# Low-half rotary scores on 128 rows of TensorE instead of 64

## The chip, the core and the metric

The kernel runs on one core of a Trainium2 chip, in one launch. The metric is the device time of one execution in microseconds (us), the median of several runs. TensorE does the matrix products (PE in the profile, PEld for its weight loads), VectorE (DVE), ScalarE (ACT) and GpSimd (POOL) do the rest, and DMA queues are fed by SyncE (SP), ACT and POOL.

## What is computed

The reference is one layer of a streaming encoder trunk: latent attention, a retention branch, a merge and a convolutional feed-forward, for a prompt of 1024 tokens and for 8 samples of 16 tokens, each with a past of 256. The change is in the attention scores alone, in the part with the rotary key:

```python
def mla_scores(qn, qp, k_nope, k_pe):
    s = jnp.einsum('bqhd,bkhd->bhqk', qn, k_nope) + jnp.einsum('bqhr,bkr->bhqk', qp, k_pe)
    return s.astype(jnp.float32) * MLA_SCALE
```

There are 8 heads. The first product runs over 128 numbers a head, the second, the rotary one, over 64, with one key for all heads. The prompt is masked in chunks of 64 keys; a softmax over the keys and a product with the values follow.

## The kernel before

Every float32 operand is split into a high half, rounded to the format that TensorE takes (fp32r), and a low half, the rest. A product of two such operands is three products: high by high, high by low, low by high. All go through one helper, `mmul` (line 188), so most rows of the profile name that line. They sum up in a bank of PSUM.

The work goes in stages: gates, latent and retention; queries, keys and values; the samples' attention; the prompt's attention; then merge and feed-forward. The two middle ones matter here.

**Rotary operands.** The rotary part has only 64 rows a head, so the query keeps both halves in one block of 128 rows: for an even head the high half lies in rows 0 to 63 and the low half in rows 64 to 127, for an odd head the other way round (`qs`, the third plane of `aq`; `qsp` for the samples). The rotary key lies twice below itself in both of its halves: `ks1` is the key's high half on rows 0 to 63 and again on 64 to 127, `kls` its low half likewise (both planes of `kpe`; `kp[0]` and `kp[1]` for the samples). One product of `qs` and `ks1` over 128 rows therefore gives query high by key high and query low by key high together. The third one, query high by key low, takes from `qs` and `kls` only the 64 rows in which the query's high half lies.

**Prompt's attention** (lines 1043 to 1131). For each head four pairs of 128-query blocks are done in the order 0, 3, 1, 2. For block i the keys are the first 128(i+1). Up to 512 keys they lie in one bank (`sc`), above that in two of half the length each. A block's scores are five products for each bank: three with the non-rotary parts (`ak`, `aq`), then the rotary one on 128 rows and the rotary one on 64 rows, both `sc<-kpe,aq` in the profile. So a head has 12 products on 64 rows: one in each of four blocks, two in a row in each of the other four. After the scores VectorE masks (line 1126), takes the row's maximum (L1058) and later scales by the reciprocal of the sum (L1069), and ScalarE takes the exponential (L1065). The result `ap` is transposed on TensorE (`apt`, L1081), split into halves `apT` (L205 on ACT, L206 on DVE), and multiplied by the values `av` into `apo`. An object `stream` places the steps of a pair behind the scores of later blocks, so that TensorE has scores to do while a softmax runs. The order is fixed when the program is written out, and each engine works through its own list.

**Samples' attention** (lines 894 to 1040). For each of 8 samples the product of the latent past and the key weights is made (`mm<-whi,lT`), and the scores of all heads against 272 keys (`sample`, from line 939): the non-rotary ones into `pn`, the rotary ones into `pp`, again one product on 128 rows and one on 64, `sm<-kp,qsp` in the profile. The next sample's products follow on TensorE.

Of the kernel before, what the change touches and what calls it, by code (L numbers as in the profile page):

```python
# [142 lines left out]


class _Stream:
    """Emits chains of dependent stages between units of matrix products."""

    def __init__(self):
        self.now, self.queue = 0, []
# [23 lines left out]
def _body(tc, d):  # L173
# [13 lines left out]
    def mmul(out, l, r, start, stop):  # L187
        E.matmul(out, l, r, start=start, stop=stop)  # L188
# [5 lines left out]
        mmul(out, ll, rh, False, stop)  # L194

    def behind():
        """What is traced in this block issues behind what ACT and DVE were given before it."""
        block = ExitStack()
        for e in (mybir.EngineType.Activation, mybir.EngineType.DVE):
            block.enter_context(tc.issue_after(next(i for i in reversed(nc.cur_bb.bb.instructions) if i.engine == e)))  # L200
        return block
# [9 lines left out]
    with ExitStack() as top:  # L211
# [105 lines left out]
            E.matmul(pw, ones, ones, start=True, stop=True)  # L317
        warm.close()

# [1 line left out]
        qside = ExitStack()  # L321
        with ExitStack() as ph:
            rows = ph.enter_context(pool("xrows"))
# [21 lines left out]
            def xk(k, t):  # L345
                return tuple(a[:, t * P:(t + 1) * P] for a in xr[k])

            # branch gates
            gside = ExitStack()
            gp = gside.enter_context(pool("gside", side=right))  # L350
            ivb = gp.tile([P, T], F32, name="ivb")
            with ExitStack() as sec:
# [14 lines left out]
                pp = [[mm.tile([P, 512], F32, name="mm") for _ in range(NCH)] for _ in range(2)]  # L367
# [39 lines left out]
                for f in range(2, 13):  # L407
                    gate_out(f, fm_tile(mm, wslot(d["w_gate"][f], D), xr))

            # latent and rope key  # L410
            with ExitStack() as sec:
                wk = sec.enter_context(pool("kvwork", bufs=2))
                mm = sec.enter_context(pool("mm_a", bufs=6, space=PSUM))
# [58 lines left out]
                stream.drain()  # L472
                A.dma_start(s_kpe, kpT.bitcast(F32))

            # retention
            with ExitStack() as sec:
                wk = sec.enter_context(pool("rwork", bufs=2))
                mm = sec.enter_context(pool("mm_b", bufs=4, space=PSUM))
# [109 lines left out]
                stream.drain()  # L588
            gside.close()

            # query latent
            qp = qside.enter_context(pool("qlat", side=right))
            qr = [(qp.tile([P, T], F32R, name=f"qlh{k}"), qp.tile([P, T], F32R, name=f"qll{k}")) for k in range(6)]
            invq = const.tile([P, NT], F32, name="invq")
# [19 lines left out]
                            A.activation(acc[:, cs], ps[c], AF.Square)  # L614
                        split(qr[f][0][:, cs], qr[f][1][:, cs], ps[c], gc(C_QLAT, f))

# [1 line left out]
        with ExitStack() as ph:  # L618
            wx = ph.enter_context(pool("wx2", bufs=2))
            pers = ph.enter_context(pool("pers"))  # L620
# [270 lines left out]

            cside.close()

            # attention of the samples
            with ExitStack() as sec:
                mm = sec.enter_context(pool("mm_s", bufs=4, space=PSUM))
                sm = sec.enter_context(pool("sm_s", bufs=4, space=PSUM))
# [41 lines left out]
                nk = PAST + NS  # L939

                def sample(b, lT, kp, rk):
                    pn = sm.tile([P, 512], F32, name="sm")
                    pp = sm.tile([P, 512], F32, name="sm")
                    for l in range(4):
                        qab = tuple(fl(a[:, l, b]) for a in qa)
                        mm3(pn[:, :nk], qab, tuple(a[:, l] for a in lT), l == 0, l == 3)
                    qb = fl(qsp[:, b])
                    mmul(pp[:, :nk], qb, kp[0], True, False)
                    mmul(pp[:, :nk], qb[0:64], kp[1][0:64], False, True)
                    own = wk.tile([P, P], F32, name="own")  # L950
                    G.memset(own, 0.0)
                    r = raw(d["lat_tm"][b].rearrange("p a c -> p (a c)"), 1024)
                    lt = tuple(wk.tile([P, 2, KVL], F32R, name=f"lt{i}") for i in range(2))
                    split(lt[0].rearrange("p a c -> p (a c)"), lt[1].rearrange("p a c -> p (a c)"), r)
                    yield 2
                    pr = sm.tile([P, 512], F32, name="sm")
                    for t2 in range(2):
                        bcast_cols(rk[:, t2], pr[:, t2 * P:(t2 + 1) * P])
                    rb = wk.tile([P, nk], F32, name="srb", bufs=1)
                    A.copy(rb[:, :PAST], pr[:, :PAST])  # L960
                    G.tensor_copy(rb[:, PAST:], rb8[:, b * NS:(b + 1) * NS])
                    s = wk.tile([P, nk], F32, name="ss_")
                    V.tensor_tensor(out=s, in0=pn[:, :nk], in1=rb, op=ALU.mult)
                    V.tensor_tensor(out=s, in0=pp[:, :nk], in1=s, op=ALU.add)
                    st = wk.tile([P, 4], F32, name="sst")
                    V.tensor_reduce(st[:, 0:1], s, AX.X, ALU.max, negate=True)
                    A.activation(s, s, AF.Exp, bias=st[:, 0:1], accum_out=st[:, 1:2])
                    V.reciprocal(st[:, 2:3], st[:, 1:2])
                    V.tensor_scalar(out=s[:, :PAST], in0=s[:, :PAST], scalar1=st[:, 2:3], scalar2=None, op0=ALU.mult)
                    G.tensor_scalar(out=own[:, b * NS:(b + 1) * NS], in0=s[:, PAST:], scalar1=st[:, 2:3], scalar2=None, op0=ALU.mult)  # L970
                    yield 3
                    pt = sm.tile([P, 512], F32, name="sm")
                    for a in range(3):
                        E.transpose(pt[:, a * P:(a + 1) * P], s[:, a * P:(a + 1) * P] if a < 2 else own, ident)
                    pT = tuple(wk.tile([P, 3, P], F32R, name=f"spT{i}", bufs=1) for i in range(2))
                    done[:] = [split(pT[0], pT[1], pt[:, :CH].rearrange("p (a c) -> p a c", a=3))]
                    yield 1
                    ps = sm.tile([P, 512], F32, name="sm")
                    for a in range(2):
                        mm3(ps, tuple(x[:, a] for x in pT), tuple(x[:, a] for x in lt), a == 0, False)  # L980
                    mm3(ps, tuple(x[:, 2] for x in pT), (ck8h, ck8l), False, True)
                    t1 = wk.tile([P, KVL], F32, name="st1", bufs=1)
                    A.copy(t1, ps)
                    yield 1
                    pt = sm.tile([P, 512], F32, name="sm")
                    for a in range(4):
                        E.transpose(pt[:, a * P:(a + 1) * P], t1[:, a * P:(a + 1) * P], ident)
                    pv = pt.rearrange("p (l h i) -> p l h i", l=4, h=H)
                    own = slice(b * NS, (b + 1) * NS)
                    split(t1T[:, :, :, 0, own], t1T[:, :, :, 1, own], pv)  # L990
# [3 lines left out]
                for b in range(NB):  # L994
# [6 lines left out]
                    kp = tuple(wk.tile([P, nk], F32R, name=f"kp{i}") for i in range(2))  # L1001
# [38 lines left out]
                A.dma_start(s_att[:, :, SEQ:].rearrange("h p c -> p h c"), at8)  # L1040
            pre.close()

# [1 line left out]
        with ExitStack() as ph:  # L1044
            ps_s = ph.enter_context(pool("ps_s", bufs=4, space=PSUM))
            ps_t = ph.enter_context(pool("ps_t", bufs=4, space=PSUM))
# [52 lines left out]
            for h in range(H):  # L1099
                qt = ld.tile([P, 3, SEQ], F32R, name="aq")  # L1100
                kt = ld.tile([P, 2, SEQ], F32R, name="ak")
                vt = ld.tile([P, 2, 8, P], F32R, name="av")
                G.dma_start(qt, s_q[h // 2][:, :, h % 2])
                G.dma_start(kt, s_k[h // 4][:, :, h % 4])
                for i in range(2):
                    G.dma_start(vt[:, i], s_v[h // 4][:, i, :, (h % 4) * P:(h % 4 + 1) * P])
                qh, kh, qs = (qt[:, 0], qt[:, 1]), (kt[:, 0], kt[:, 1]), qt[:, 2]
                vh = (vt[:, 0].rearrange("p a c -> p (a c)"), vt[:, 1].rearrange("p a c -> p (a c)"))
                at = wk.tile([P, SEQ], F32, name="aat")
                order = (0, 3, 1, 2)  # L1110
                for g in order:
                    pm = []
                    for i in (2 * g, 2 * g + 1):
                        nk = (i + 1) * P
                        cs = [(0, nk)] if nk <= 512 else [(0, nk // 2), (nk // 2, nk)]
                        sc = [ps_s.tile([P, 512], F32, name="sc") for _ in cs]
                        qi = slice(i * P, (i + 1) * P)
                        e = slice(64 * (h % 2), 64 * (h % 2) + 64)
                        for n, (l, ks) in enumerate(((qh[0], kh[0]), (qh[0], kh[1]), (qh[1], kh[0]), (qs, ks1), (qs, kls))):
                            for c, (a, b) in enumerate(cs):  # L1120
                                if n < 4:
                                    mmul(sc[c][:, :b - a], l[:, qi], ks[:, a:b], n == 0, False)
                                else:
                                    mmul(sc[c][:, :b - a], l[e, qi], ks[e, a:b], False, True)
                        a, b = cs[-1]
                        V.memset(sc[-1][0:64, b - a - 64:b - a], -1e30)
                        pm.append(soft(i, sc, cs))
                        if i % 2:
                            stream.start(values(h, g, pm, vh, at, g == order[-1]))
                        stream.tick()  # L1130
            stream.drain()

# [1 line left out]
        rp = top.enter_context(pool("rrows", side=right))  # L1134

        def new_rows(mm, w, f0, f1, fill):
# [20 lines left out]
        with ExitStack() as ph:  # L1157
# [37 lines left out]
            layer(mm, "w_oa", 8, lambda k, hi, lo: split(hi, lo, raw(s_att[k], T)), att_out)  # L1195
            layer(mm, "w_out", 8, lambda k, hi, lo: split(hi, lo, xf[k]), res_out)

            # the up projection starts before its norm is known
            hr, (pg, pv) = new_rows(mm, "w_up", 0, NJ, lambda k, hi, lo: split(hi, lo, xf[k], gc(C_FFN, k)))

# [1 line left out]
        with ExitStack() as ph:  # L1202
            wk = ph.enter_context(pool("fwork", bufs=1))
            cn = cst("s_conv", (P, NF, 18), wk)
# [169 lines left out]
```

## Time and profile before

| | |
|---|---|
| median of 3 runs | 2484.79 us (2482.94 to 2485.39) |
| span of the profiled execution, first to last instruction | 2481.9 us |
| products on TensorE (PE), busy | 2453.8 us, 99% |
| VectorE, ScalarE, GpSimd, busy | 53%, 34%, 12% |
| samples' attention, steady part | 1015 to 1130 us |
| prompt's attention | 1149.8 to 1345 us |
| one head of the prompt in the middle of it | 1267.80 to 1292.15 us, 24.35 us |

The profile gives the span of the profiled execution and no other time of it; the median of the runs lies 2.9 us above that span. A busy PE is not a PE at its peak: a product's end in the trace is modelled, and the next one's start may lie before it. What a product costs in a dense stretch is the step from its start to the next one's start. In a row of the time line, "x3" is three instructions of one kind put together, with the start of the first and the time to the end of the last, and "64\*128 64x384" is a product whose weights have 64 rows and 128 columns and which streams 64 rows by 384 columns. In brackets stands the idle time of that engine before the row, and what ended it.

### The profile page before, as it was taken

How to read it: one execution, taken by the hardware profiler on the slowest of the kernel's cores; microseconds unless marked ns; L12 is line 12 of the kernel's file. 1: busy time of each engine (PE TensorE's matmuls, PEld its weight loads, DVE VectorE, ACT ScalarE, POOL GpSimd, SP SyncE). 2: the span in 40 equal slices, each digit the busy share in tenths (PEclk: the TensorE clock that was granted, in tenths of full speed). 3: DMA queues.
4: the chain of work that ended last, by engine and by line, in shares of the span. 5: the costliest groups of instructions: out<-in, count | busy, mean ns of one | idle time of the engine just before them, and what ended most of it. 6: DMA issues, size and time to landing. Idle time of an engine off the chain costs nothing.

```text
span 2481.9 us, 36197 instructions
## 1 busy us (share of the span) xinstructions
PE 2453.8 (99%) x14360; PEld 2327.1 (94%) x14360; DVE 1319.7 (53%) x2779; ACT 836.9 (34%) x2050; POOL 302.0 (12%) x514
## 2 busy tenths in 40 slices
PE   9999999999999999999999999999999999999999
PEld 8999898998999978887888999999999999999999
DVE  5223456446249766445776244346555555555555
ACT  5121332333236545665555122133222122222220
POOL 0001000001013312332110000001110101101010
PEclk9999999999999999999999999999999999999999
DMA  5333220111226676328663342211111111111102
GB/s 199 102 110 111 85 71 20 64 64 37 69 78 181 188 245 207 130 84 234 163 177 105 124 161 91 91 60 43 51 43 43 43 43 35 51 43 43 41 29 84
DMA packets 125273, 238.52 MB, mean 96 GB/s; under 512 B 10000, under 2 KB 73872, under 8 KB 124848
## 3 DMA queue, kind: packets, MB, share of 16 engines
q1 hardware_dynamic: 40320, 125.95, 15.5%
q10 hardware_dynamic: 58256, 62.30, 7.4%
q0 software_dynamic: 26528, 47.95, 7.0%
q8 instruction: 113, 1.85, 0.3%
q14 instruction: 56, 0.46, 0.1%
HBM read 168.76 MB, written 67.42 MB: 95 GB/s over the span
## 4 chain that ended last, share of the span: by engine, by line
PE 95%; DVE 3%; ACT 1%; DMA 1%; issue 1%; POOL 0%; ACTq 0%; SPq 0%; DVEq 0%; POOLq 0%
PE mm L188 81%; PE sm L188 4%; PE sc L188 4%; PE apo L188 2%; PE apt L1081 2%; DVE wlo L206 0%; PE sm L554 0%; PE sm L311 0%; PE sm L691 0%; DVE uqT L697 0%; DMA wraw<-s_att 0%; ACT whi L205 0%; PE sm L859 0%; DMA wraw<-w_gate 0%; DVE uqT L209 0%
## 5 line engine op out<-in xcount | busy, mean ns | idle before, releaser
L205 ACT CAST whi<-wraw 128x1024 fp32r<-128x1024 f32 (+2 forms) x165 | 172.4, 1053 | 725.7 <-PE mm L188 623.9
L188 PE MATMUL mm<-rh,whi 128*128 128x384 f32 x1728 | 393.0, 336 | 1.6 <-ACT rh L205 1.5
L188 PE MATMUL mm<-rh,wlo 128*128 128x384 f32 x1680 | 384.2, 336 | 0.0
L188 PE MATMUL mm<-rl,whi 128*128 128x384 f32 x1632 | 372.7, 336 | 0.1
L188 PEld LDWEIGHTS mm<-rh,whi 128*128 128x128 f32 x1728 | 308.2, 188 | 3.5 <-ACT rh L205 1.7
L188 PEld LDWEIGHTS mm<-rh,wlo 128*128 128x128 f32 x1680 | 300.3, 188 | 0.0
L188 PEld LDWEIGHTS mm<-rl,whi 128*128 128x128 f32 x1632 | 291.1, 188 | 0.4 <-DVE rl L206 0.4
L206 DVE TENSOR_TENSOR wlo<-wraw,whi 128x1024 fp32r<-128x1024 f32 (+2 forms) x165 | 200.1, 1222 | 141.8 <-ACT whi L205 141.8
L188 PE MATMUL mm<-whi,xh 128*128 128x256 f32 (+2 forms) x720 | 228.4, 334 | 0.7 <-DVE gsig L361 0.7
L188 PE MATMUL mm<-whi,xl 128*128 128x256 f32 (+2 forms) x720 | 225.5, 330 | 0.0
L188 PE MATMUL mm<-wlo,xh 128*128 128x256 f32 (+2 forms) x720 | 225.0, 329 | 0.2 <-DVE wlo L206 0.2
L1258 DVE TENSOR_TENSOR xf<-mm,xf 128x384 f32<-128x384 f32 x264 | 131.5, 550 | 86.2 <-PE mm L188 86.2
L1232 DVE TENSOR_TENSOR u<-mm,iv2b 128x384 f32<-128x384 f32 (+1 forms) x126 | 57.1, 507 | 208.9 <-PE mm L188 208.9
L188 PEld LDWEIGHTS mm<-whi,xl 128*128 128x128 f32 x720 | 132.6, 190 | 12.1
L188 PEld LDWEIGHTS mm<-whi,xh 128*128 128x128 f32 x720 | 132.7, 190 | 10.5 <-issue 0.7
L188 PEld LDWEIGHTS mm<-wlo,xh 128*128 128x128 f32 x720 | 132.8, 190 | 9.8 <-DVE wlo L206 0.4
L188 PE MATMUL mm<-xh,whi 128*128 128x384 f32 x528 | 123.6, 340 | 3.8 <-ACT whi L205 3.0
L188 PE MATMUL mm<-xl,whi 128*128 128x384 f32 x528 | 121.9, 336 | 0.0
L188 PE MATMUL mm<-xh,wlo 128*128 128x384 f32 x528 | 121.4, 336 | 0.0
L188 PE MATMUL mm<-ah,whi 128*128 128x384 f32 x480 | 110.5, 336 | 0.0
L188 PE MATMUL mm<-al,whi 128*128 128x384 f32 x480 | 110.4, 336 | 0.0
L188 PE MATMUL mm<-ah,wlo 128*128 128x384 f32 x480 | 109.8, 336 | 0.0
(448 smaller groups left out, 4450.1 us busy)
## 6 DMA issues: line engine op xcount, KB each, us to landing
wraw<-w_up SPq DMA_DIRECT2D x44, 512.0 KB, 3.2
s_q<-uqT ACTq DMA_DIRECT2D x36, 384.0 KB, 3.1
aq<-s_q POOLq DMA_DIRECT2D x8, 1536.0 KB, 9.3
wraw<-w_dn SPq DMA_DIRECT2D x22, 512.0 KB, 3.2
s_gate<-gsig ACTq DMA_DIRECT2D x16, 576.0 KB, 4.9
mg<-s_gate POOLq DMA_DIRECT2D x16, 576.0 KB, 4.6
wraw<-w_rqkv SPq DMA_DIRECT2D x16, 512.0 KB, 3.8
s_v<-kvT ACTq DMA_DIRECT2D x16, 512.0 KB, 4.7
```

What stands on the lines that cost most here:

```text
L188: E.matmul(out, l, r, start=start, stop=stop)
L205: A.copy(hi, src)
L206: return V.tensor_tensor(out=lo, in0=src, in1=hi.bitcast(F32), op=ALU.subtract)
L1081: E.transpose(pt[:, j * 256 + e * P:j * 256 + (e + 1) * P], pm[e][:, jj * P:(jj + 1) * P], ident)
L1232: V.tensor_tensor(out=u[:, 2 + c * CH:2 + c * CH + n], in0=ps[c][:, :n], in1=ivb[:, c * CH:c * CH + n], op=ALU.mult)
L1258: V.tensor_tensor(out=xf[f][:, cs], in0=ps[c], in1=xf[f][:, cs], op=ALU.add)
```

## The change

In both places the last of the five products takes all 128 rows, instead of the 64 on which the query's high half lies. What is added to the scores by it is query low by key low. The number of products is the same, and so are their columns; 104 of them, 96 in the prompt's attention and 8 in the samples', have 128 rows in place of 64. On each engine the instructions stand in the same order in both kernels. Comment lines taken out aside, this is the whole of it:

```diff
@@ sample
                     mmul(pp[:, :nk], qb, kp[0], True, False)
-                    mmul(pp[:, :nk], qb[0:64], kp[1][0:64], False, True)
+                    mmul(pp[:, :nk], qb, kp[1], False, True)
@@ attention of the prompt
                         qi = slice(i * P, (i + 1) * P)
-                        e = slice(64 * (h % 2), 64 * (h % 2) + 64)
                         for n, (l, ks) in enumerate(((qh[0], kh[0]), (qh[0], kh[1]), (qh[1], kh[0]), (qs, ks1), (qs, kls))):
                             for c, (a, b) in enumerate(cs):
-                                if n < 4:
-                                    mmul(sc[c][:, :b - a], l[:, qi], ks[:, a:b], n == 0, False)
-                                else:
-                                    mmul(sc[c][:, :b - a], l[e, qi], ks[e, a:b], False, True)
+                                mmul(sc[c][:, :b - a], l[:, qi], ks[:, a:b], n == 0, n == 4)
```

## Rows read from the trace of the kernel before

**Rows 1.** The profile's page: the busy time of each engine, and the chain of work that ended last, by engine.

```profile
PE 2453.8 (99%) x14360; PEld 2327.1 (94%) x14360; DVE 1319.7 (53%) x2779; ACT 836.9 (34%) x2050; POOL 302.0 (12%) x514
...
PE 95%; DVE 3%; ACT 1%; DMA 1%; issue 1%; POOL 0%; ACTq 0%; SPq 0%; DVEq 0%; POOLq 0%
```

**Rows 2.** Busy time in stretches, in us, with the number of instructions, then the granted clock of TensorE as a share of its full speed, the DMA share and GB/s: the samples' steady part, the prompt's first head, one head in the middle, and the prompt's whole stage.

```profile
1015.00:1130.00 115.00, 115.00 (x565) 94.25 (x563) 45.84 (x111) 72.34 (x294) 39.92 (x74) 1.00 0.25 82
...
1149.80:1174.00 24.20, 24.09 (x149) 19.62 (x148) 18.96 (x63) 12.83 (x41) 2.59 (x4) 1.00 1.29 380
...
1267.80:1292.15 24.35, 24.35 (x158) 20.26 (x158) 18.14 (x59) 14.18 (x43) 3.25 (x4) 1.00 0.64 173
1149.80:1345.00 195.20, 194.75 (x1242) 161.57 (x1242) 145.91 (x466) 112.70 (x336) 20.89 (x26) 1.00 0.63 170
```

**Rows 3.** Groups of weight loads by shape: busy us, mean ns of one, then the idle time of the loading side just before them and what ended it.

```profile
L188 PEld LDWEIGHTS sc<-kpe,aq 128*128 128x128 f32 x96 | 17.7, 188 | 1.3
L188 PEld LDWEIGHTS sc<-kpe,aq 64*128 64x128 f32 x96 | 15.3, 184 | 15.1 <-issue 13.4
```

**Rows 4.** Time line around the block with 384 keys of the head in the middle: first the products from the rotary one on 128 rows on, with the first and the second product of the values behind it (the last row holds the second and the third), then the weight loads of the same stretch.

```profile
1279.82 0.34 PE L188 MATMUL sc<-kpe,aq 128*128 128x384 f32 x1
1280.08 0.44 PE L188 MATMUL sc<-kpe,aq 64*128 64x384 f32 x1
1280.45 0.39 PE L188 MATMUL apo<-apT,av 128*128 128x256 f32 x1
1280.68 0.40 PE L188 MATMUL apo<-apT,av 128*128 128x256 f32 x2
...
1279.64 0.19 PEld L188 LDWEIGHTS sc<-kpe,aq 128*128 128x128 f32 x1
1280.08 0.18 PEld L188 LDWEIGHTS sc<-kpe,aq 64*128 64x128 f32 x1 [0.25 <-issue]
1280.45 0.76 PEld L188 LDWEIGHTS apo<-apT,av 128*128 128x128 f32 x6 [0.19 <-ACT ap L1065]
```

**Rows 5.** Time line of the products around the block with 768 keys of the same head (two banks of 384), from the second rotary product on 128 rows to the first transposes; the last row begins with the second transpose.

```profile
1287.43 0.34 PE L188 MATMUL sc<-kpe,aq 128*128 128x384 f32 x1
1287.69 0.44 PE L188 MATMUL sc<-kpe,aq 64*128 64x384 f32 x1
1287.97 0.34 PE L188 MATMUL sc<-kpe,aq 64*128 64x384 f32 x1
1288.24 0.33 PE L1081 MATMUL apt<-ident,ap 128*128 128x128 f32 x1
1288.40 0.38 PE L1081 MATMUL apt<-ident,ap 128*128 128x128 f32 x2
```

**Rows 6.** The same for the block with 512 keys in one bank: the last two products on 128 rows and, with the one on 64 and the first transpose left out between them, the row that begins with the second transpose.

```profile
1281.71 0.40 PE L188 MATMUL sc<-ak,aq 128*128 128x512 f32 x1
1281.94 0.40 PE L188 MATMUL sc<-kpe,aq 128*128 128x512 f32 x1
...
1282.87 0.38 PE L1081 MATMUL apt<-ident,ap 128*128 128x128 f32 x2
```

**Rows 7.** The same for one sample: its rotary products and the first two products of the next sample's past.

```profile
1080.39 0.29 PE L188 MATMUL sm<-kp,qsp 128*128 128x272 f32 x1
1080.61 0.39 PE L188 MATMUL sm<-kp,qsp 64*128 64x272 f32 x1
1080.93 0.50 PE L188 MATMUL mm<-whi,lT 128*128 128x512 f32 x1
1081.26 0.40 PE L188 MATMUL mm<-wlo,lT 128*128 128x512 f32 x1
```

**Rows 8.** Time line of dense stretches in which all products have 128 rows: three products of 384 columns and the start of the next three (merge stage), 24 products of the values and the scores behind them, and two products of 128 columns with the start of the next.

```profile
1349.79 0.68 PE L188 MATMUL mm<-rh,wlo 128*128 128x384 f32 x3
1350.31 0.68 PE L188 MATMUL mm<-rl,whi 128*128 128x384 f32 x3
...
1288.98 3.00 PE L188 MATMUL apo<-apT,av 128*128 128x256 f32 x24
1291.82 0.50 PE L188 MATMUL sc<-ak,aq 128*128 128x128 f32 x3
...
1267.60 0.39 PE L188 MATMUL sc<-ak,aq 128*128 128x128 f32 x2
1267.82 0.28 PE L188 MATMUL sc<-kpe,aq 128*128 128x128 f32 x1
```

**Rows 9.** Time line of VectorE in the same head: the mask of the block with 1024 keys, the first step after its scores, and the scaling of that block's softmax, the last step before its transposes.

```profile
1277.45 0.11 DVE L1126 MEMSET sc<- 64x64 f32 x1
...
1281.22 0.80 DVE L1069 TENSOR_SCALAR ap<-ap,ast 128x1024 f32<-128x1024 f32 x1
```

**Rows 10.** Waits of the loading side of TensorE (what it waited for, us in total, times, longest): on VectorE's split of the transposed softmax in the prompt's first head (1149.8 to 1174 us), and the same after the last head's scores (1340 to 1346 us).

```profile
PEld apo L188 <- DVE apT L206: 0.3, 1, 0.3
...
PEld apo L188 <- DVE apT L206: 0.5, 1, 0.5
```

**Rows 11.** Stretches as in Rows 2: before and in a stretch at the lower clock, at the end of the keys' stage, and the samples' last chain.

```profile
985.00:990.40 5.40, 3.42 (x31) 3.22 (x30) 3.24 (x9) 1.78 (x5) 3.32 (x4) 1.00 0.72 243
990.46:1000.70 10.24, 7.66 (x28) 6.57 (x28) 4.81 (x7) 6.13 (x11) 1.81 (x11) 0.50 0.78 244
...
1130.00:1142.50 12.50, 7.63 (x36) 4.88 (x35) 6.66 (x13) 4.19 (x9) 3.88 (x5) 1.00 0.49 164
```

## The prediction

> **What bounds the kernel now.** The page comes first: TensorE is busy for 99% of the span and makes up 95% of the chain that ended last [rows 1]. A busy share says little of an engine whose records overlap, so the second view is the two stages that the change touches, by stretches [rows 2]. In the samples' steady part TensorE is busy for 115.00 of 115 us, in the prompt's stage for 194.75 of 195.20, at the full clock. VectorE comes next: 145.91 of 195.20 us in the prompt's stage, and 18.14 of 24.35 in one head. So time taken off TensorE is taken off the kernel as long as the softmax on VectorE and ScalarE keeps up.
>
> The third view is the weight loads by shape [rows 3]. The 96 loads on 64 rows have 15.1 us of idle time before them, 13.4 of it with nothing that the profile shows to wait for; the 96 on 128 rows, one product earlier, have 1.3. Nothing was late there: TensorE itself stood between two kinds of product.
>
> The fourth view is the time line there [rows 4]. The load for the 128-row product begins at 1279.64, and the product at 1279.82. The 64-row load comes only at 1280.08, 0.25 us after the last load ended, and its product begins in the same moment. The next load, on 128 rows again, waits another 0.19 us, and its product, too, begins with it at 1280.45. The profile puts this second wait down to ScalarE's `ap`, which fits nothing that the values need; the same wait stands before the transposes [rows 5] with no releaser. Both ways across the border, from 128 rows to 64 and back, a load does not start beneath the product before it.
>
> **The change, part by part.** It removes no product and no column. It takes away 72 visits to the other shape: 64 in the prompt (8 heads by 8 blocks; two products on 64 rows in a row are one visit) and 8 in the samples.
>
> *What one visit costs.* I take the time from the start of the last 128-row product to the start of the second product after the visit, less what the same products take where all have 128 rows. The prices for that: 384 columns take (1350.31 - 1349.79) / 3 = 0.173 us, 256 columns (1291.82 - 1288.98) / 24 = 0.118, 128 columns (1267.82 - 1267.60) / 2 = 0.11 [rows 8], and 512 columns 1281.94 - 1281.71 = 0.23 [rows 6].
> - One bank of 384, values behind it [rows 4]: 1280.68 - 1279.82 = 0.86; two products of 384 and one of 256 are 2 x 0.173 + 0.118 = 0.46; the visit costs 0.40.
> - Two banks of 384, transposes behind them [rows 5]: 1288.40 - 1287.43 = 0.97; three of 384 and one of 128 are 0.63; the visit costs 0.34.
> - One bank of 512, transposes behind it [rows 6]: 1282.87 - 1281.94 = 0.93; two of 512 and one of 128 are 0.57; it costs 0.36.
> - A sample [rows 7]: 1081.26 - 1080.39 = 0.87; two of 272 columns, at 0.173 / 384 a column 0.12 each, and one of 512 are 0.48; it costs 0.39.
>
> Half of the prompt's visits have two banks (0.34), half one (0.36 to 0.40, mean 0.38), so I take 0.36: 64 x 0.36 = 23.0 us. The samples give 8 x 0.39 = 3.1. Together 26.1 us on TensorE. The bounds are 72 x 0.34 = 24.5 and 72 x 0.40 = 28.8.
>
> *What the full rows add.* Afterwards the low product has the shape and the weights of the one before it, and that one's step is the price used above, so I add nothing. No row has the new product itself; the bound from above stands with the last rival.
>
> *A rule that speaks against it.* In the rows the load for a 128-row product begins at 1279.64, while the scores before it, on 128 rows as well, still run, and the product follows 0.18 us after the one before, about the bare step for 384 columns [rows 4, 8]. The Trainium skill (TensorE: Matmul & The Clock Gate, Part 3, The mechanism) says instead that a weight load overlaps a running product only where the two use different groups of rows; by it, loads would stay in the open after the change, with the time of the third rival below in place of the forecast. The trace disagrees with it.
>
> *What is not passed on.* The saving counts where TensorE is the one that is waited for. Four places are not so:
> - Each of the seven later heads: the block with 1024 keys is scaled until 1281.22 + 0.80 = 1282.02 [rows 9] and transposed from 1282.87 on [rows 6], a slack of 0.85 us. The chain begins with the mask at 1277.45 [rows 9], and two visits lie between (0.40 and 0.36, [rows 4, 6]), so 0.76 of the 0.85 is eaten. It should just do, but VectorE is the busiest helper there, 18.14 of then some 21.5 us [rows 2]; I take 0.2 a head, 7 x 0.2 = 1.4, between 0 and 7 x 0.76 = 5.3.
> - The first head: VectorE is busier than later, 18.96 of 24.20 us [rows 2], and TensorE already waits for its split, 0.3 us once [rows 10], so part of its 8 x 0.36 = 2.9 goes into that wait; I take 1.0, between 0 and 2.9.
> - The samples' last chain is one of latencies: TensorE is busy for 7.63 of 12.5 us [rows 11]. The eighth visit lies at its start; I take 0.3 of its 0.39 as lost, between 0 and 0.39.
> - Behind the last scores TensorE waits 0.5 us for the split [rows 10]; I take 0.3, between 0 and 0.5.
>
> Together 3.0 us are lost, so 26.1 - 3.0 = 23.1 us are gained: 2481.9 - 23.1 = 2458.8 for the profiled span, and 2484.8 - 23.1 = 2461.7 for the median, which lies 2.9 us above that span. Everything behind the prompt's stage moves up by the same amount: the next rows are split by ScalarE behind its last copy of `apo`, and TensorE waits for them as before.
>
> With the bounds of the visits and of the losses (0 to 9.1), the forecast's own range is 28.8 to 24.5 - 7.0 = 17.5 us of gain, all losses at their worst at once being left out: 2456.0 to 2467.3.
>
> **The rivals.**
> - *The softmax sets the pace.* If VectorE and ScalarE come no faster than now, the block with 1024 keys loses its whole 0.76 in seven heads, and the pair with 640 and 768 keys, which has the next most work on VectorE, as much again: 7 x 1.52 = 10.6 in place of 1.4. Gain 26.1 - 10.6 - 1.6 = 13.9, time 2470.9. For it: VectorE at 75% of the stage, and in order. Against it: it has 6 us of idle time in a head, and its work begins earlier, too. 8%.
> - *The clock falls in the samples' last chain.* The granted clock was 0.50, the lower level of 1.2 GHz, for 10.24 us after a stretch in which TensorE was busy for 3.42 of 5.40 us [rows 11]. The samples' chain, busy for 7.63 of 12.5 us, kept 1.00. It will come 3 us earlier, and its gaps may then fall otherwise. Such a fall would cost at most half of 10.24 us, 5.1: time 2466.8. 6%.
> - *Loads stay in the open.* The load of the low product and the one behind it may go on waiting for the product before them, since they share its rows. Then of each visit two loads of a step of 0.11 remain, 0.36 - 0.22 = 0.14, and 72 x 0.14 = 10.1: time 2474.7. Against it: the 128-row load at 1279.64 [rows 4]. 3%. This is what the Trainium skill's rule, weighed above, would make of it.
> - *The wait doesn't come from the shape* but from the end of a sum in PSUM, which lies at the same product. Then nothing changes: 2484.8. Against it: where the values end and scores begin, both on 128 rows, there is no gap (24 steps of 0.118 reach right to the scores' start, [rows 8]). 3%.
> - *Slower: the wait stays for such a reason, and a product's time goes by its rows.* The 64-row products have 8 x 4608 + 8 x 272 = 39040 columns, at 0.173 / 384 a column 17.6 us; if half the rows had taken half of that, the change adds 8.8 us: 2493.6. It decides wherever a visit gives back less than 8.8 / 72 = 0.12 us. Against it: two 64-row products of 384 columns stand 0.28 us apart [rows 5], not 0.09. 3%.
>
> **How the numbers follow.** The forecast has 77%. Its range to 2467.3 takes in the clock's case as well, 83% together; for the softmax, I stretch it to 2469, short of that rival's full price. A measurement of this kernel can tell 0.2%, 5 us, from no change; all cases but the last two are faster by more: 94% faster, 3% the same, 3% slower.
>
> **What would show it.** In the changed kernel's trace the loads `sc<-kpe,aq` and `sm<-kp,qsp` have one shape each, with 1 to 3 us of idle time before all 192 of the prompt's. The step from the rotary product to the low one is 0.17 to 0.18 us at 384 columns, and one head takes about 24.35 - 2.7 = 21.7 us in place of 24.35. The prompt's stage takes about 195.2 - 20.3 = 175 us, and each sample's period is 0.4 us shorter. The forecast is wrong if waits of TensorE for `ap` or `apT` take over in the middle heads (first rival), if PEclk shows 0.5 near 1130 to 1150 us (second), if the idle time before the low product's load stays (third and fourth), or if its step is longer than that of the product before it (last).

## The result and the profile after

The changed kernel takes 2464.56 us, median of 4 runs (2463.86 to 2468.71), against 2484.02 us for the kernel before, run beside it (2482.94 to 2485.39, 4 runs). The ratio is 0.9925, with a 95% interval from 0.9910 to 0.9939: 19.5 us faster, where 23.1 were forecast. The profiled run took 2464.82 us, its span is 2463.0 us, 18.9 less than before.

The page first: the busy time of each engine, and the chain that ended last. They are the same lines as in [rows 1].

```profile
PE 2435.9 (99%) x14360; PEld 2333.8 (95%) x14360; DVE 1319.5 (54%) x2779; ACT 835.8 (34%) x2050; POOL 302.3 (12%) x514
...
PE 94%; DVE 3%; ACT 1%; DMA 1%; issue 1%; POOL 0%; ACTq 0%; SPq 0%; DVEq 0%; POOLq 0%
```

TensorE is busy for 17.9 us less with the same 14360 products, and the other engines do what they did. The groups of weight loads by shape show where:

```profile
L188 PEld LDWEIGHTS sc<-kpe,aq 128*128 128x128 f32 x192 | 33.5, 188 | 2.6
...
L188 PEld LDWEIGHTS sm<-kp,qsp 128*128 128x128 f32 x16 | 2.5, 188 | 0.0
```

All loads have one shape. In [rows 3] 16.4 us of idle time stood before the prompt's 192; now it is 2.6.

The next rows are the counterpart of [rows 4, 5, 7]: the time line of the block with 384 keys in a head in the middle (products, then loads), of the two banks of 384 in the same head, and of one sample.

```profile
1267.91 0.34 PE L188 MATMUL sc<-kpe,aq 128*128 128x384 f32 x1
...
1268.08 0.35 PE L188 MATMUL sc<-kpe,aq 128*128 128x384 f32 x1
...
1268.38 0.40 PE L188 MATMUL apo<-apT,av 128*128 128x256 f32 x2
...
1267.91 0.19 PEld L188 LDWEIGHTS sc<-kpe,aq 128*128 128x128 f32 x1
...
1268.09 0.19 PEld L188 LDWEIGHTS apo<-apT,av 128*128 128x128 f32 x1
...
1274.49 0.51 PE L188 MATMUL sc<-kpe,aq 128*128 128x384 f32 x2
...
1275.12 0.38 PE L1081 MATMUL apt<-ident,ap 128*128 128x128 f32 x2
...
1046.34 0.29 PE L188 MATMUL sm<-kp,qsp 128*128 128x272 f32 x1
...
1046.83 0.40 PE L188 MATMUL mm<-wlo,lT 128*128 128x512 f32 x1
```

From the rotary product to the low one the step is 0.17 us. From the rotary product to the second product of the values it is 1268.38 - 1267.91 = 0.47 us, where [rows 4] had 0.86 and the forecast's bare steps add up to 0.46. Of the two banks, the row at 1274.49 begins with the second rotary product and the one at 1275.12 with the second transpose: 0.63 us for 0.97 in [rows 5], and again just the bare steps. In the sample it is 0.49 for 0.87 [rows 7]. The loads for the low product and for the values now begin at 1267.91 and 1268.09, each while the product before it runs. A rule that the Trainium skill states (TensorE: Matmul & The Clock Gate, Part 3, The mechanism), that loads overlap running products only where the groups of rows differ, would have them wait; as in the trace of before, these rows say otherwise.

Where the prompt's stage begins and ends, and where two of its heads lie, is read from single products in the time line, in the changed kernel

```profile
1151.36 0.27 PE L188 MATMUL sc<-ak,aq 128*128 128x128 f32 x1
...
1169.54 0.27 PE L188 MATMUL sc<-ak,aq 128*128 128x128 f32 x1
...
1256.81 0.28 PE L188 MATMUL sc<-ak,aq 128*128 128x128 f32 x1
...
1278.53 0.28 PE L188 MATMUL sc<-ak,aq 128*128 128x128 f32 x1
...
1329.16 0.45 PE L188 MATMUL mm<-rh,whi 128*128 128x384 f32 x1 [1.51 <-ACT rh L205]
```

and in the kernel before:

```profile
1149.91 0.27 PE L188 MATMUL sc<-ak,aq 128*128 128x128 f32 x1
...
1169.63 0.28 PE L188 MATMUL sc<-ak,aq 128*128 128x128 f32 x1
...
1347.77 0.44 PE L188 MATMUL mm<-rh,whi 128*128 128x384 f32 x1 [1.51 <-ACT rh L205]
```

The stage, from its first scores to the merge's first product, went from 197.86 us to 177.80, 20.06 less; the forecast had 20.3. The first head takes 18.18 us instead of 19.72, the head in the middle 21.72 instead of 24.35 [rows 2]. Yet the stage **begins later** than before, though the eight samples ahead of it have become shorter. The stretches between them, in the columns of [rows 2], show why: first in the kernel before, from the last sample's first rotary product to the prompt's first scores,

```profile
1129.48:1149.91 20.43, 15.56 (x103) 12.55 (x101) 9.64 (x17) 7.53 (x16) 8.00 (x10) 1.00 0.85 224
```

then in the changed kernel, as a whole and in parts:

```profile
1126.22:1151.36 25.14, 20.11 (x102) 16.49 (x101) 9.79 (x17) 7.54 (x16) 8.01 (x10) 0.73 0.87 232
...
1126.50:1130.00 3.50, 1.90 (x11) 1.34 (x10) 1.80 (x6) 0.91 (x3) 1.01 (x1) 1.00 0.00 0
1130.07:1140.31 10.24, 8.23 (x22) 5.44 (x20) 4.25 (x7) 2.85 (x6) 1.99 (x3) 0.50 0.64 204
1140.31:1143.72 3.41, 1.99 (x15) 1.76 (x16) 0.69 (x1) 0.59 (x1) 2.21 (x3) 1.00 0.98 334
1143.72:1147.13 3.41, 3.41 (x18) 3.41 (x17) 0.42 (x1) 0.37 (x1) 2.80 (x4) 0.50 1.47 310
```

The samples' last chain arrives 3.26 us earlier (2.7 from seven shorter periods; the other 0.5 lie ahead of the samples, where the program is the same) and then takes 4.71 us longer. The granted clock, 1.00 throughout this chain in the kernel before, is 0.50 in 13.65 of these us, the lower level of 1.2 GHz. It fell twice, each time behind a stretch in which TensorE was busy for little more than half (1.90 of 3.50 us, 1.99 of 3.41). The products show the price one by one:

```profile
1130.85 0.63 PE L188 MATMUL sm<-ck8h,spT 128*128 128x512 f32 x1
1131.28 0.63 PE L188 MATMUL sm<-ck8l,spT 128*128 128x512 f32 x1
1131.70 0.63 PE L188 MATMUL sm<-ck8h,spT 128*128 128x512 f32 x1
```

512 columns take 0.43 us from start to start here, and took 0.23 in [rows 6].

So the profile adds up to - 3.26 + 4.71 - 20.06 = - 18.6 us, and 0.3 us more were saved behind the prompt.

### The profile page after: what moved, and what is told of

Its sections match the earlier page's. It is cut to its first block, busy times and chain, and to the rows that moved or that the text cites. A ratio compares the mean times of both kernels' runs of the same rounds, so it can differ in the third digit from the quotient of the medians.

```text
span 2463.0 us, 36197 instructions
## 1 busy us (share of the span) xinstructions
PE 2435.9 (99%) x14360; PEld 2333.8 (95%) x14360; DVE 1319.5 (54%) x2779; ACT 835.8 (34%) x2050; POOL 302.3 (12%) x514
## 4 chain that ended last, share of the span: by engine, by line
PE 94%; DVE 3%; ACT 1%; DMA 1%; issue 1%; POOL 0%; ACTq 0%; SPq 0%; DVEq 0%; POOLq 0%
PE mm L188 81%; PE sm L188 4%; PE sc L188 3%; PE apo L188 2%; PE apt L1081 1%; DVE wlo L206 0%; DMA s<-s_ret 0%; PE sm L554 0%; DVE uqT L697 0%; DMA wraw<-w_gate 0%; PE sm L311 0%; PE sm L691 0%; PE sm L859 0%; DVE uqT L209 0%; PE sm L987 0%
```

## The experiments

The ratio is to the kernel before, run beside each (median 2484.56 us for e1 to e4, 2484.41 for full_again, e5, e8 and e9, 2485.02 for e10), with a 95% interval. "Chain" is the time from the last sample's first rotary product to the prompt's first scores, "stage" from there to the merge's first product, both in the profiled run.

| | median us | runs | ratio | chain | stage |
|---|---|---|---|---|---|
| before (first profile) | | | | 20.43 | 197.86 |
| after (first profile) | 2464.56 | 4 | 0.9925 (0.9910 to 0.9939) | 25.14 | 177.80 |
| full_again: the changed kernel | 2464.39 | 4 | 0.9922 (0.9909 to 0.9935) | 24.86 | 177.80 |
| e1_prompt_only | 2464.33 | 5 | 0.9920 (0.9908 to 0.9933) | 22.02 | 177.81 |
| e2_samples_only | 2486.84 | 11 | 1.0009 (1.0000 to 1.0018) | 26.01 | 197.96 |
| e4_two_visits | 2495.82 | 5 | 1.0045 (1.0031 to 1.0059) | 21.98 | 210.2 |
| e5_second_place | 2487.41 | 11 | 1.0014 (1.0005 to 1.0022) | 20.39 | 200.9 |
| e3_fill | 2462.46 | 4 | 0.9913 (0.9899 to 0.9926) | 22.45 | 178.7 |
| e8_fill_four | 2461.38 | 4 | 0.9910 (0.9897 to 0.9923) | 21.93 | 177.6 |
| e10_fill_three | 2459.79 | 4 | 0.9897 (0.9880 to 0.9913) | 20.12 | 177.78 |
| e9_before_fill | 2484.03 | 12 | 0.9999 (0.9990 to 1.0007) | 20.85 | 197.9 |

### The two parts apart

The prompt's part alone is the changed kernel with the samples' line as before:

```diff
-                    mmul(pp[:, :nk], qb, kp[1], False, True)
+                    mmul(pp[:, :nk], qb[0:64], kp[1][0:64], False, True)
```

> The prompt's low rotary product runs on 128 rows, the samples' one stays on 64. Theory (a visit to the 64-row shape costs TensorE 0.36 us, and the changed kernel lost 4.7 us again because its samples' last chain came 3 us earlier and met the lower clock): the prompt's stage gives its 20 us, the samples' periods stay as in the kernel before, and the last chain of the samples keeps the granted clock of 1.00, so 2484 - 20 = 2464 us, as fast as the full change although only 64 of 72 visits are gone. Rival 1 (the clock falls there whatever the samples do, since the prompt's part or the run decides it): 2468 to 2469 us, with 0.50 near 1130 to 1150 us. Rival 2 (the prompt's saving depends on the samples' stage): another step than 20 us from the prompt's first scores to its last.

The samples' part alone is the kernel before with the opposite edit.

> The samples' low rotary product runs on 128 rows, the prompt's one stays on 64. Theory: each sample's period is 0.39 us shorter, the last chain comes 3 us earlier, the clock falls to 0.50 in it, and 4.7 us are given back: 2484 - 3 + 4.7 = 2485.5 us, no faster or slower than before by 1 to 2 us. Rival (the fall has nothing to do with the samples' shift): clock 1.00 in the chain and 2481 us.

The changed kernel ran once more:

> The changed kernel once more, on the chip of the next two, as their yardstick. Theory: 2464.5 us, with the clock at 0.50 in the samples' last chain in most executions. Rival (that fall was of the one profiled execution): 2460 us and 1.00.

The prompt's part alone gives the whole gain: 2484.56 - 2464.33 = 20.2 us, with a stage as short as in the changed kernel. The samples' part alone gives none: by the medians it is 2.3 us slower (the interval begins at no change), although it makes the seven periods before the chain 2.7 us shorter in all. Its 11 runs lie between 2481.01 and 2490.49 us. The stretches of its profile, from the fall of the clock to the prompt's first scores:

```profile
1129.55:1146.62 17.07, 13.64 (x47) 10.41 (x46) 5.21 (x9) 3.81 (x8) 6.99 (x9) 0.50 0.91 256
1146.62:1151.60 4.98, 4.98 (x45) 4.98 (x45) 2.59 (x4) 2.54 (x4) 0.00 (x0) 1.00 1.63 374
```

Here two thirds of the chain ran at the lower clock, and it took 26.01 us. In the second profile of the changed kernel the clock fell three times, for 3.4 us each:

```profile
1124.81:1128.00 3.19, 1.59 (x11) 1.12 (x10) 1.29 (x4) 1.18 (x4) 1.01 (x1) 1.00 0.00 0
1128.00:1131.42 3.42, 3.42 (x9) 2.19 (x7) 1.41 (x5) 0.61 (x2) 1.25 (x2) 0.50 0.00 0
1131.42:1134.83 3.41, 1.94 (x11) 1.21 (x11) 1.38 (x3) 1.55 (x3) 0.00 (x0) 1.00 0.85 263
1134.83:1138.24 3.41, 3.06 (x7) 1.86 (x7) 2.05 (x2) 0.26 (x1) 0.74 (x1) 0.50 0.92 291
```

(and again from 1141.66 to 1145.07). The chain's 24.86 us are close to the 25.14 of the first profile, with another pattern. In the profile of the prompt's part alone it fell once, behind a longer stretch at the full clock in which TensorE was busy for two thirds:

```profile
1128.52:1142.90 14.38, 9.50 (x49) 6.47 (x48) 6.82 (x13) 4.52 (x11) 5.22 (x7) 1.00 0.52 170
1142.91:1146.33 3.42, 3.42 (x18) 3.42 (x17) 0.42 (x1) 0.37 (x1) 2.77 (x4) 0.50 1.11 374
```

In this kernel nothing ahead of that chain is changed, and its chain takes 1.6 us longer than in the profile of before. So the clock is not wholly a matter of the program. But in the three profiles with the samples' part the chain takes 4.4 to 5.6 us more than the 20.43 of before; in the three more without it (e1, e4, e5), between nothing and 1.6.

These are single executions. The mean granted clock of a whole run is on record for nearly all runs, and though it takes in falls elsewhere, too, it says the same: 0.990 to 0.994 (median 0.992) in the 8 runs of the changed kernel and 0.991 to 0.995 (0.992) in the 11 of the samples' part, but 0.993 to 0.995 (0.995) in the 5 of the prompt's part and 0.993 to 0.997 (0.994) in 45 of the kernel before. The fastest run of the samples' part, 2481.01 us, had 0.995: it is the time that the rival had forecast for a chain at the full clock.

### Is it the number of visits?

Here the kernel before is changed so that the rotary part goes bank by bank, and blocks with two banks have two visits to the 64-row shape instead of one. The products are the same:

```diff
-                        for n, (l, ks) in enumerate(((qh[0], kh[0]), (qh[0], kh[1]), (qh[1], kh[0]), (qs, ks1), (qs, kls))):
+                        for n, (l, ks) in enumerate(((qh[0], kh[0]), (qh[0], kh[1]), (qh[1], kh[0]))):
                             for c, (a, b) in enumerate(cs):
-                                if n < 4:
-                                    mmul(sc[c][:, :b - a], l[:, qi], ks[:, a:b], n == 0, False)
-                                else:
-                                    mmul(sc[c][:, :b - a], l[e, qi], ks[e, a:b], False, True)
+                                mmul(sc[c][:, :b - a], l[:, qi], ks[:, a:b], n == 0, False)
+                        for c, (a, b) in enumerate(cs):
+                            mmul(sc[c][:, :b - a], qs[:, qi], ks1[:, a:b], False, False)
+                            mmul(sc[c][:, :b - a], qs[e, qi], kls[e, a:b], False, True)
```

> The kernel before, with the two banks of a long block done one after the other in the rotary part, so that the two 64-row products of a block are no longer next to each other: 104 visits in place of 72, the same 104 products. Theory (each visit costs 0.34 to 0.40 us): 32 x 0.36 = 11.5 us more, 2495.5 us. Rival (each 64-row product costs, whatever stands beside it, as 26 / 104 = 0.25 us): no change, 2484 us. Second rival (the wait belongs to the end of a sum in a bank): no change either, since each bank's sum ends once in both.

The median rose by 2495.82 - 2484.56 = 11.3 us for 32 more visits, 0.35 us each; the stage of the profile, by 12.3 us, gives 0.38. The groups of loads by shape:

```profile
L188 PEld LDWEIGHTS sc<-kpe,aq 128*128 128x128 f32 x96 | 18.0, 188 | 7.2 <-issue 6.4
...
L188 PEld LDWEIGHTS sc<-kpe,aq 64*128 64x128 f32 x96 | 17.5, 183 | 21.8 <-issue 20.1
```

Before both, the idle time is longer than in [rows 3], and before the 128-row loads it is new: those of the second banks now follow a 64-row product. With the same products and columns as before, the cost goes by the crossings.

### Is it the end of a sum?

Here the 64-row product of the kernel before becomes the second of the five instead of the last:

```diff
-                        for n, (l, ks) in enumerate(((qh[0], kh[0]), (qh[0], kh[1]), (qh[1], kh[0]), (qs, ks1), (qs, kls))):
+                        for n, (l, ks) in enumerate(((qh[0], kh[0]), (qs, kls), (qh[0], kh[1]), (qh[1], kh[0]), (qs, ks1))):
                             for c, (a, b) in enumerate(cs):
-                                if n < 4:
-                                    mmul(sc[c][:, :b - a], l[:, qi], ks[:, a:b], n == 0, False)
+                                if n != 1:
+                                    mmul(sc[c][:, :b - a], l[:, qi], ks[:, a:b], n == 0, n == 4)
                                 else:
-                                    mmul(sc[c][:, :b - a], l[e, qi], ks[e, a:b], False, True)
+                                    mmul(sc[c][:, :b - a], l[e, qi], ks[e, a:b], False, False)
```

> The kernel before, with the prompt's low rotary product still on 64 rows, but as the second of the five products of a block instead of the last, so that the sum in a bank ends with a product on 128 rows. Theory (the wait belongs to the change of shape): still one visit a block, each with products on 128 rows on both sides, 64 x 0.38 in place of 64 x 0.36: 2484.5 + 1 = 2485.5 us, no faster than before. Rival (the wait belongs to the end of a sum in PSUM): the 64-row product no longer lies there, the wait goes with its place and the price of the shape vanishes: up to 20 us less, 2464 us.

It took 2487.41 us, 3.0 more than before. The idle time before the 64-row loads moved with them into the middle of the sum:

```profile
L188 PEld LDWEIGHTS sc<-kpe,aq 128*128 128x128 f32 x96 | 17.7, 188 | 1.3
...
L188 PEld LDWEIGHTS sc<-kpe,aq 64*128 64x128 f32 x96 | 15.4, 184 | 14.2 <-issue 12.7
```

A sum now ends with a product on 128 rows, and nothing was saved. So the end of a sum is not the cause. The 3.0 us appear in the stage as well (200.9 for 197.86), and spread over the 64 visits they are 0.05 us each. In the block with two banks of 384, from the second product on 128 rows to the second one behind the visit:

```profile
1290.00 0.34 PE L188 MATMUL sc<-ak,aq 128*128 128x384 f32 x1
...
1291.09 0.33 PE L188 MATMUL sc<-ak,aq 128*128 128x384 f32 x1
```

These four steps of 384 columns take 1.09 us, 0.40 more than the bare 0.69, where the visit with transposes behind it cost 0.34 in the kernel before. What makes a visit dearer with scores behind it is not shown.

### Giving the clock back

If the samples' last chain lost its time to the clock, and the clock falls behind TensorE's gaps, filling these gaps with products should return it. In what is left of the last two samples' chains, 20 products of 512 columns on operands that lie in SBUF anyway go to spare banks of PSUM; nobody reads their result, and the outputs are the same. The three versions differ in the number of spare tiles N alone:

```diff
                     for t2 in range(2):
                         bcast_cols(rk[:, t2], pr[:, t2 * P:(t2 + 1) * P])
+                        fill(b, 3 - t2)
...
                         E.transpose(pt[:, a * P:(a + 1) * P], s[:, a * P:(a + 1) * P] if a < 2 else own, ident)
+                    fill(b, 3 if b == NB - 1 else 0)
...
                     mm3(ps, tuple(x[:, 2] for x in pT), (ck8h, ck8l), False, True)
+                    fill(b, 3)
...
                         E.transpose(pt[:, a * P:(a + 1) * P], t1[:, a * P:(a + 1) * P], ident)
+                    fill(b, 6 if b == NB - 1 else 0)
...
+                def fill(b, n):
+                    if b >= NB - 2 and spare:
+                        for i in range(n):
+                            mmul(spare[i % N], c8h[:, 0], ck8h, True, True)
...
                     stream.start(sample(b, lT, kp, rk))
+                    if b == NB - 1:
+                        spare.extend(mm.tile([P, 512], F32, name="mm") for _ in range(N))
```

First with one tile:

> The full change, with 20 products of 512 columns whose result nobody reads, put on TensorE in the waits of the samples' last chain. Theory (the gaps of TensorE in that chain bring the clock down): with the gaps filled the granted clock stays at 1.00 from 1126 to 1150 us, and 4 to 4.7 us come back: 2460 us, 4 us faster than the full change. Rival 1 (the fall does not follow TensorE's gaps): 0.50 again, 2465 us. Rival 2 (the filling products, 0.22 us each, delay the chain more than the clock gives back): clock 1.00, but the chain longer by up to 20 x 0.22 = 4.4 us: 2464 us.

It took 2462.46 us. The clock stayed at 1.00 while the chain ran, and fell only behind it:

```profile
1126.00:1129.50 3.50, 3.12 (x17) 2.31 (x15) 1.89 (x6) 0.85 (x2) 1.01 (x1) 1.00 0.00 0
...
1149.64:1153.05 3.41, 3.41 (x11) 3.04 (x10) 1.78 (x7) 0.75 (x4) 0.00 (x0) 0.50 1.08 406
```

The spare tile had also changed which bank of PSUM the prompt's first scores take. TensorE now waited 2.04 us for VectorE's copy (line 1051) of the last of the four sums ahead of them, which stands behind the split of a weight: that sum's bank was the one they took. So the same fills went over four tiles:

> The full change with the same 20 filling products, spread over four tiles in place of one. In the first filled kernel the one tile shifted the order of the PSUM banks behind it, so that the prompt's first scores waited 2.04 us for a bank that VectorE still read, and the clock fell for 3.4 us right there. Theory: with four tiles the banks come in the old order, this wait and this fall go, the chain keeps 1.00, and the whole 4.7 us come back: 2459.5 to 2460.5 us. Rival (the wait is for the first head's key load, which lands no earlier): no gain on the first filled kernel, 2462.5 us.

2461.38 us, with the clock at 1.00 to the end of the chain; the changed kernel beside it took 2464.39. The expectation that the banks would come in the old order did not hold: the wait remained, now on the third of the four sums.

```profile
1126.75:1148.68 21.93, 18.86 (x122) 16.04 (x120) 10.49 (x19) 7.78 (x17) 9.11 (x12) 1.00 0.92 230
...
1148.68 0.33 PE L188 MATMUL sc<-ak,aq 128*128 128x128 f32 x1 [1.53 <-DVE wraw L1051]
```

With three tiles it should be the second sum's bank:

> The changed kernel with the same 20 filling products in the samples' last chain as in the run with four spare tiles, now over three. Nothing else differs; the results of the filling products go nowhere. What moves is the bank in which the prompt's first scores land: with four spare tiles it was the bank of the third sum behind the attention's output weights, whose copy on VectorE stands behind the split of a weight that landed late, and TensorE waited 1.7 us there; with three it is the bank of the second sum, copied some 4 us earlier. Theory: that wait goes and the first scores come right behind the last sums, at the full clock: the time falls from 2461.4 by 1.0 to 1.7 us, to 2459.7 to 2460.4, about what the prediction's terms give without any fall of the clock (2459.9). Rival 1: the second block's scores, which need the bank of the third sum, take the wait over: no change, 2461.0 to 2461.8. Rival 2: the clock falls once behind the chain as in the run with one spare tile: 2462 to 2463, with 0.50 for 3.4 us between 1145 and 1155.

2459.79 us, as the theory had it. The wait is gone; the first row below is the chain's stretch, the others its first product, the first scores and the stage's end:

```profile
1126.35:1146.47 20.12, 18.57 (x123) 15.93 (x121) 9.73 (x17) 7.44 (x16) 8.01 (x10) 1.00 0.85 224
...
1126.35 0.29 PE L188 MATMUL sm<-kp,qsp 128*128 128x272 f32 x1
...
1146.47 0.28 PE L188 MATMUL sc<-ak,aq 128*128 128x128 f32 x1
...
1324.25 0.45 PE L188 MATMUL mm<-rh,whi 128*128 128x384 f32 x1 [1.51 <-ACT rh L205]
```

The chain takes 20.12 us, 5.0 less than in the changed kernel's first profile, at the full clock. This version is faster than both kernels: by 25.2 us than the one before (ratio 0.9897), and by some 4.7 us than the changed one, whose 8 runs lie between 2463.30 and 2468.71 us; the 4 here lie between 2458.14 and 2460.40, though the two did not run side by side.

The control is the kernel before with the fills of e8_fill_four:

> The kernel before with the same 20 filling products on four tiles. Theory (they do nothing but hold the clock, and it was held there already): 2484.5 us, within 1.5 us of before. Rival (the filling itself makes the stage faster or slower, so that the filled kernels say nothing of the clock): off by 3 to 5 us.

2484.03 us, ratio 0.9999: no change, and the chain 20.85 us for 20.43. The 0.4 us more are about the wait for a bank that four tiles bring, 0.46 us here.

```profile
1129.54:1150.39 20.85, 19.18 (x122) 16.07 (x120) 10.37 (x19) 7.83 (x17) 8.15 (x11) 1.00 0.90 226
```

So the fills gain nothing by themselves; what they give the changed kernel is what the clock had taken from it.

## Why the prediction was right, point by point

- **The cause** is shown: it is the change of shape. Without it the idle time before the loads is gone, with 32 more changes it costs 32 times 0.35 us, and at another place in the sum it stays.
- **The price of a visit** was forecast as 0.36 us in the prompt and 0.39 in a sample. The three time lines after the change show the bare steps to within 0.01 us, and the added visits gave 11.3 us / 32 = 0.35. In the samples it came out: six of the seven periods shrank from 16.37 to 15.98 us. In the prompt it was a little too high: the head in the middle gave 24.35 - 21.72 = 2.63 us for its 8 visits, 0.33 each. The block with 384 keys, at 0.40 the dearest, had stood for too many others.
- **What the full rows add**, nothing: the low product's step is 0.17 us, that of its neighbour. The "slower" rival is refuted by it, and loads that stay in the open by the 2.6 us that are left.
- **What is not passed on in the prompt**: forecast 1.0 us in the first head, 1.4 in seven others, 0.3 behind the last scores, so 23.0 - 2.7 = 20.3 saved; measured 20.06. That this fits is in part luck, since two terms were too large and make up for each other. The first head gave 1.54 us, less than the 1.9 forecast. A head in the middle gave 2.63, close to the forecast 2.7, but as cheaper visits with next to nothing lost, not as 8 x 0.36 less 0.2. The loads do wait there, in seven places:

```profile
PEld apt L1081 <- ACT ap L1065: 1.3, 7, 0.2
...
1269.32 0.79 DVE L1069 TENSOR_SCALAR ap<-ap,ast 128x1024 f32<-128x1024 f32 x1
...
1269.88 0.39 PE L188 MATMUL sc<-kpe,aq 128*128 128x512 f32 x1
...
1270.12 0.27 PE L1081 MATMUL apt<-ident,ap 128*128 128x128 f32 x1
...
1270.25 0.30 PE L1081 MATMUL apt<-ident,ap 128*128 128x128 f32 x1
```

The first row adds up the waits of the loading side from 1180 to 1318 us. The others are from the head in the middle: the scaling of the block with 1024 keys, which ends at 1269.32 + 0.79 = 1270.11, the last score product of the block with 512 keys, and the first two transposes. The first transpose comes after a bare step; the second, the first to take from the scaled block, comes 1270.25 - 1270.12 = 0.13 us later, where 0.11 is bare. So of the 0.2 us that the loading side waits, the products lose some 0.02 a head, less than 0.2 us in seven heads in place of 1.4.
- **The softmax as the new pace** did not come: from 1180 to 1318 us these 1.3 us are all the waits that the profile shows for TensorE.
- **The samples' last chain** is the term that was mis-sized. The sum took 0.3 of the eighth visit's 0.39 us as lost, so the chain should have become 0.09 us shorter; it became 4.71 longer, since the second rival came true on top of the forecast, and close to its price (5.1). That price had some luck in it: the lower level lasted 13.65 us, not 10.24, but TensorE was not busy all that time. The rival had been given 6%, because a single profile of before showed the chain at the full clock with TensorE busy for 7.63 of 12.5 us. The prediction did say that the chain moves by 3 us and that its gaps may then fall otherwise. It did not weigh that one profile says little of a clock that differs from execution to execution, nor that the stretch of [rows 11] with a fall behind it was, at 3.42 of 5.40 us, no less busy than this chain; the clock should have had a chance nearer to a half.
- **The time**: the span was forecast as 2458.8 us and came to 2463.0. These 4.2 more are the chain's 4.8 less small gains elsewhere. The median missed by only 2.9 (2464.56 for 2461.7), and the difference is luck: the forecast put 2.9 us between span and median, where the changed kernel has 1.6. A run's time lies 1.7 to 1.9 us above its own span wherever both are on record; the 2.9 held besides that the profiled execution of before was a quick one. The range to 2467.3 held the median since it was wide enough for the clock's case. Where the fills keep the clock up, the span is 2458.6 us, for the forecast 2458.8.

Two things stay open. Whether the lower clock falls on the chain is not settled by the program alone, as the 1.6 us in e1_prompt_only and the three patterns show; the runs do not tell why the samples' part makes it so much likelier. That it is the shift of 3 us is a guess. And why a visit in the second place of a sum costs 0.05 us more than one at its end is not shown.

## What to carry to other kernels

Where TensorE is the bound, look at the shapes of neighbouring products: a product on fewer rows between full ones cost 0.33 to 0.40 us a visit here, some twice the 0.17 us of a product of 384 columns, and filling up the rows cost nothing. Read it from the time between starts across the border, less the bare steps, and count visits, not products. Read a wait of the loading side against the steps of the products beside it: 0.2 us there were some 0.02 us of TensorE's time. And when a saving moves up a stretch in which TensorE has gaps, look at the granted clock there, in more than one profile: it took back 4.7 us of some 24 here, and 20 products that nobody reads held it up.

## What the runs showed of the hardware

- The clock took back 4.7 us in a chain that came 3 us earlier. In three profiles with the samples' part the lower level covered 13.65, 10.24 and 17.07 us of the chain in three different patterns; the first two are of one and the same kernel. The Trainium skill (TensorE: Matmul & The Clock Gate, Part 1, What's actually happening) says of the products at a kernel's start that the number of slow ones varies from run to run for the same kernel; in these two profiles the same holds in the middle of one.
- The Trainium skill (TensorEngine Tiling (Array Packing), Key Properties) says that a change of tiling mode drains TensorE. If a product on 64 rows between products on 128 counts as such a change, the trace agrees: the loads on both sides of it begin only with their own product [rows 4]. Here it has a price, 0.35 us for going over to 64 rows and back.
- Spare tiles moved the prompt's first scores to another bank of PSUM, and with it a wait to TensorE: 2.04 us with one, 1.53 with four, none with three. The medians were 2462.46, 2461.38 and 2459.79 us; with one tile the clock fell behind the chain as well.
